# Modulation products on GpSimd and ScalarE beside the filter transforms, and the low parts of x on VectorE one product later

## The chip, the cores and the metric

The kernel runs on one core of one Trainium2 chip. The metric is the device time of one execution in microseconds (us); three timed runs of the kernel before gave a median of 2732.48 us (2732.22 to 2733.73). One further execution was recorded with the hardware profiler. The engines are named as the profile names them: PE is TensorE's matmuls, PEld its weight loads, DVE is VectorE, ACT is ScalarE, POOL is GpSimd (Pool), SP is SyncE, which issues most of the DMAs.

## What is computed

One block of a hybrid encoder on 512 tokens of width 2048, in float32. What matters here is its beginning: six modulation vectors from a condition, the first of which scale and shift the input; long filters that are made from positions; and the first projection.

```python
cond = silu(c)
mod  = cond @ w_ada + b_ada               # (2048) @ (2048 x 12288)
sh1, sc1, g1, sh2, sc2, g2 = split(mod, 6)
h = x * (1 + sc1) + sh1                   # 512 x 2048
z = h @ w_in + b_in                       # 2048 x 9216
# z feeds a spatial gating unit, a Hyena branch and two gates;
# the Hyena branch convolves with long filters
filt = hyena_filters(512, ...)            # a small MLP of sines, times a window
k_spec = spectrum(filt forward, filt backward)   # one for each of 2 orders
# then: branches, gates, w_o, layer norm, a 2048-8192-2048 MLP, layer norm
```

Only `sh1` and `sc1`, 2 x 2048 values, are needed before the first projection. Each value is a dot product of `cond` (2048) with a column of `w_ada`.

## The kernel before

**Products in three parts.** Large products are made as three products of 32-bit operands that are split in a high part and a low part: high times high, high times low, low times high. ScalarE rounds to the high part (`hi`), another engine subtracts it from the original to get the low part (`lo`). Weights are loaded in blocks of 128 x 1024 (512 KB), ScalarE makes `whi` (line 164, `cast`), VectorE makes `wlo` (line 169, `finish`). A block is 24 matmuls of 128 x 128 by 128 x 512.

**The modulation dot products.** `w_ada` is stored transposed, so that 128 outputs lie on the partitions and 1024 of the 2048 inputs along the row. An *item* is such a tile of 128 x 1024 (512 KB); a column group `kc` of 128 outputs needs four items (shift and scale, two halves each), and there are 16 groups, so 64 items before the first projection is complete. `Modulation.load` issues the DMA of the next item into one of two kinds of buffer: up to eight "early" ones in the pool `actp`, which is shared with the modulated input and shrinks as that fills, and a ring of three (`araw`). `Modulation.step` takes the oldest item, multiplies it with `cond` and sums it up in one VectorE instruction (line 289), and issues one more load. After every fourth step `first_input` runs for the next `kc`: Pool adds the two halves and the bias (`mod_sum`, lines 295 and 296, 128 x 2 elements each), ScalarE makes the high part of the modulated input and the modulated input itself in place (lines 476 and 477, 128 x 512), and Pool subtracts the two to get the low part (line 478).

**The filters.** `flt` makes the spectra in eight iterations (the loop over `n`, lines 547 to 566). In iteration `n`, PE makes the taps of part `n+1` (`taps`, line 435, 12 to 14 matmuls into four PSUM banks) and then the transform of part `n` (lines 360 to 372, 12 matmuls into four banks). ScalarE copies one of these banks (line 362). VectorE multiplies the taps of `n+1` with a window (`windowed`, line 445, four instructions, one operand in PSUM) and then makes sums and differences of the transform (`sums`, lines 376 to 381, six instructions, one operand in PSUM). With all eight banks in use, the taps of part `n+2` have to wait for `windowed(n+1)`, and the transform of `n+1` for `sums(n)`. In iterations 0, 2 and 4 `parts` splits the next filter weights, the low part on VectorE (line 77, 128 x 512). In each iteration VectorE also does two modulation steps, so that 20 of the 64 items are done when the loop ends.

**The first projection.** The loop over `u` (lines 574 to 591, 16 blocks of `w_in`) then interleaves, in VectorE's order, three or four modulation steps, the `wlo` of the next block (`finish`), and on PE the 24 matmuls of the present block, until at `u` = 12 all 64 items are done. After it come the short convolutions (lines 487 to 491) and the rest of the block, where PE works with little idle time to the end.

**The order.** Nothing is reordered: every engine and every DMA queue carries out its instructions in the order in which the program issues them, and waits on semaphores for the operands and buffers of each. An instruction that waits holds up all behind it on its engine.

Of the kernel before, what the change touches and what calls it, by code (L numbers as in the profile page):

```python
# [13 lines left out]
AF = mybir.ActivationFunctionType  # L14
OP = mybir.AluOpType
# [25 lines left out]
def block_kernel(ctx: ExitStack, tc: tile.TileContext, t):  # L41
    nc = tc.nc
# [11 lines left out]
    def slot(name, dt=F32):  # L54
        return heap.tile([P, 512], dt, name=name, tag="slot")
# [4 lines left out]
    def act_pair(kc):  # L60
        both = actp.tile([P, 1024], F32R, name=f"act{kc}", tag="act")
        return both[:, 0:512], both[:, 512:1024]
# [4 lines left out]
    def f32(ap):  # L67
        return ap.bitcast(F32)

    def load(dst, src, queue=nc.sync):  # L70
        queue.dma_start(dst, src)
        return dst
# [39 lines left out]
    class Weights:  # L112


        def __init__(self):
            self.blocks = blocks()
            self.raw, self.half, self.ready, self.kept, self.used = [], [], [], {}, set()
            self.ahead, self.done, self.later, self.queue = 1, False, None, nc.sync
# [12 lines left out]
        def load(self):  # L131
            w, cg, kp = next(self.blocks, (None, 0, 0))
            if w is None:
                self.done = True
                return
            raw = wts.tile([P, 1024], F32, name="wraw", tag="wraw")
            load(raw, w[cg, kp], self.queue)
            self.raw.append((raw, (w.name, cg, kp)))
# [96 lines left out]
    def cload(name, shape, queue=nc.sync):  # L235
        return load(const.tile(list(shape), F32, name="c_" + name), t[name], queue)
# [3 lines left out]
    nc.scalar.activation(warm, warm, AF.Sigmoid)  # L240
    hw1 = cload("hw1", (EMB, HID))
    featT = load(slot("featT")[:EMB], t["featT"])
    cond = const.tile([P, D], F32, name="cond")
    for h in range(2):
# [22 lines left out]
    dots = const.tile([P, 6, KC, 2], F32, name="dots")  # L267
    mod = const.tile([P, 6, KC], F32, name="mod")

    class Modulation:  # L270
        def __init__(self, order, room=lambda: 0):

            self.order, self.raw, self.room = [(m, kc, h) for m, kc in order for h in range(2)], [], room

        def load(self):
            early = sum(r[0] for r in self.raw)
            more = early < min(self.room(), 8)
            if self.order and (more or len(self.raw) - early < 3):
                m, kc, h = self.order.pop(0)
                if more:  # L280
                    raw = actp.tile([P, 1024], F32, name="araw", tag="act")
                else:
                    raw = wts.tile([P, 1024], F32, name="araw", tag="araw")
                load(raw, t["ada"][m, kc, h])
                self.raw.append((more, raw, m, kc, h))

        def step(self):
            _, raw, m, kc, h = self.raw.pop(0)
            nc.vector.scalar_tensor_tensor(raw, raw, 1.0, cond[:, 1024 * h:1024 * (h + 1)], op0=OP.mult,  # L289
                                           op1=OP.mult, accum_out=dots[:, m, kc, h:h + 1])  # L290
            if len(self.raw) < 11:
                self.load()

    def mod_sum(m, kc, eng=nc.vector):
        eng.tensor_tensor(mod[:, m, kc], dots[:, m, kc, 0], dots[:, m, kc, 1], op=OP.add)
        eng.tensor_tensor(mod[:, m, kc], mod[:, m, kc], bada[:, m, kc], op=OP.add)
# [47 lines left out]
    class Forward:  # L344
# [30 lines left out]
        def sums(self, tiles):  # L375
            nc.vector.tensor_tensor(self.ea, self.e0, self.eo, op=OP.add)
            self.minus(self.e0, self.e0, self.eo)
            for half, e in enumerate((self.ea, self.e0)):
                o = self.o[half]
                nc.vector.tensor_tensor(tiles[half], e, o, op=OP.add)  # L380
                self.minus(tiles[2 + half], e, o)
# [86 lines left out]

    h1 = []

    def first_input(kc, xt):

        mod_sum(slice(0, 2), kc, nc.gpsimd)
        hi, lo = act_pair(kc)
        sc, sh = mod[:, 1, kc:kc + 1], mod[:, 0, kc:kc + 1]
        nc.scalar.activation(hi, xt, AF.Identity, bias=sh, scale=sc)
        nc.scalar.activation(xt, xt, AF.Identity, bias=sh, scale=sc)
        nc.gpsimd.tensor_tensor(lo, xt, f32(hi), op=OP.subtract)
        h1.append((hi, lo))

    def short_conv(ps, which, hf):
# [16 lines left out]
    ada = Modulation(((m, kc) for kc in range(KC) for m in range(2)), lambda: KC - 2 - len(h1) - 4 * bool(windows))  # L498
# [14 lines left out]
    xt = []  # L513

    def x_load():
        if len(xt) < KC:
            xt.append(load(slot("xT"), t["xT"][len(xt)]))

    done = []

    def ada_steps(n):

        for _ in range(n):
            ada.step()
            done.append(None)
            if len(done) % 4 == 0:
                first_input(len(h1), xt[len(h1)])
                x_load()

    x_load()  # L530
    ada.load()
    fc = table("fwd", 3)
    for m in (1, 4):
        nc.vector.tensor_scalar(bada[:, m], bada[:, m], 1.0, None, op0=OP.add)
    busy(14)
    ada_steps(2)
    flt.parts(0)
    flt.ready()
    busy(14)
    x_load()  # L540
    for _ in range(5):
        ada.load()
    flt.taps(0)
    ada_steps(2)
    flt.windowed(0)
    weights.later, weights.queue = [], nc.scalar
    for n in range(8):
        if n < 6 and n % 2 == 0:
            flt.fetch(n + 2)
        if n < 7:  # L550
            flt.taps(n + 1)
        sums = flt.transform(n)
        ada_steps(2)
        if n < 7:
            flt.windowed(n + 1)
        flt.store()
        if n < 6:
            flt.parts(n + 2)
        sums()
        if 2 <= n < 5:  # L560
            weights.load()
        if n == 5:
            weights.cast()
        if n == 6:
            weights.finish()
            weights.cast()
# [198 lines left out]
    ada = Modulation((m, kc) for m in (2, 4, 3, 5) for kc in range(KC))  # L765
# [77 lines left out]
    for hf in range(2):  # L843
# [5 lines left out]
        for i in range(4):  # L849
            u, n = slot("u"), 4 * hf + i  # L850
# [70 lines left out]
    r = [[None] * 4 for _ in TILES]  # L921
# [103 lines left out]
    early, late = (0, 1), (2, 3)  # L1025
# [213 lines left out]
```

## Time and profile before

| | |
|---|---|
| median of the runs | 2732.48 us |
| the profiled execution's own time | 2733.2 us |
| its span, first to last instruction | 2731.4 us |
| PE busy | 2688.6 us (98%) |
| VectorE busy | 1539.5 us (56%) |
| ScalarE busy | 777.8 us (28%) |
| Pool busy | 118.8 us (4%) |
| mean granted TensorE clock | 0.996 |

The profile's rows give times in us from the start of the span. A row of a timeline reads: start, duration, engine, line, operation, output from inputs, partitions x elements and type, and how many such instructions the row merges; in brackets how long the engine was idle before it and what ended that. A row of the table by stages gives each engine's busy time in the stretch with the count of instructions, the granted clock, and the share and rate of the DMA engines. The shares over the whole span hide that the first 200 us, where the change lies, are limited in another way than the rest.

### The profile page before, as it was taken

The numbers are of one execution on the slowest core, as the hardware profiler recorded it, in microseconds if no ns is written. First come the engines' busy times: TensorE is split into PE (matmuls) and PEld (weight loads), VectorE is DVE, ScalarE is ACT, GpSimd is POOL, SyncE is SP. The second block draws the span as 40 slices with busy tenths as digits, with TensorE's granted clock in tenths as the row PEclk, the third lists the DMA queues.
The fourth block names the chain that finished last, engine by engine and source line by source line (L and its number), as shares of the span: only waits on it lengthen the run. The fifth ranks groups of instructions, "written<-read, shape, count | busy, mean of one in ns | idle before, by whom it ended". The sixth has DMA issues, their size and how long they took to land.

```text
span 2731.4 us, 30019 instructions
## 1 busy us (share of the span) xinstructions
PE 2688.6 (98%) x12019; PEld 2210.1 (81%) x12019; DVE 1539.5 (56%) x2052; ACT 777.8 (28%) x949; POOL 118.8 (4%) x102
## 2 busy tenths in 40 slices
PE   8999999999999999999999999999999999999996
PEld 5678778888888888878988888888888888888885
DVE  8987989544575566456774343443433434334348
ACT  2343332222232222324621222312223222131232
POOL 0330000000000000140010000000000000000001
PEclk9999999999999999999999999999999999999998
DMA  9762333555665567445543222322223222223342
GB/s 346 300 242 84 118 113 135 196 190 196 200 209 186 198 220 258 156 152 177 183 134 100 94 100 93 101 93 100 94 99 97 96 100 93 101 92 101 95 140 82
DMA packets 120189, 400.49 MB, mean 147 GB/s; under 512 B 14187, under 2 KB 14283, under 8 KB 119920
## 3 DMA queue, kind: packets, MB, share of 16 engines
q1 hardware_dynamic: 116656, 387.26, 41.9%
q10 hardware_dynamic: 3392, 11.31, 1.1%
q8 instruction: 94, 1.54, 0.2%
q14 instruction: 47, 0.39, 0.0%
HBM read 388.01 MB, written 10.50 MB: 146 GB/s over the span
## 4 chain that ended last, share of the span: by engine, by line
PE 91%; DVE 5%; DMA 3%; issue 1%; ACT 1%; SPq 0%; DVEq 0%; ACTq 0%
PE d L207 57%; PE t L952 29%; DMA araw<-in_ada 2%; PE flt L435 1%; PE f_o L338 1%; DVE wlo L169 1%; DMA spec<-spec 1%; PE inv L703 1%; PE inv L690 1%; DMA wraw<-in_w_m 0%; PE f L342 0%; DVE araw L289 0%; DVE r L1104 0%; DVE r L968 0%; PE tr L609 0%
## 5 line engine op out<-in xcount | busy, mean ns | idle before, releaser
L207 PE MATMUL d<-act,whi 128*128 128x512 f32 (+1 forms) x4224 | 1273.1, 384 | 0.0
L169 DVE TENSOR_TENSOR wlo<-wraw,whi 128x1024 fp32r<-128x1024 f32 x480 | 589.0, 1229 | 993.2 <-ACT whi L164 989.9
L164 ACT CAST whi<-wraw 128x1024 fp32r<-128x1024 f32 x480 | 504.9, 1053 | 1488.2 <-PE d L207 873.2
L207 PEld LDWEIGHTS d<-act,whi 128*128 128x128 f32 x4224 | 783.1, 188 | 155.6 <-issue 2.4
L207 PE MATMUL d<-act,wlo 128*128 128x512 f32 (+1 forms) x2112 | 810.2, 384 | 10.2 <-DVE wlo L169 10.2
L207 PEld LDWEIGHTS d<-act,wlo 128*128 128x128 f32 x2112 | 396.7, 188 | 93.3 <-DVE wlo L169 15.9
L952 PE MATMUL t<-whi,fh 128*128 128x512 f32 x960 | 373.5, 389 | 0.0
L952 PE MATMUL t<-wlo,fh 128*128 128x512 f32 x960 | 373.5, 389 | 0.0
L952 PE MATMUL t<-whi,fl 128*128 128x512 f32 x960 | 373.5, 389 | 0.0
L289 DVE SCALAR_TENSOR_TENSOR araw<-araw,cond 128x1024 f32<-128x1024 f32 x192 | 238.6, 1259 | 7.8 <-DMA araw<-in_ada 7.6
L952 PEld LDWEIGHTS t<-whi,fl 128*128 128x128 f32 x960 | 180.2, 188 | 37.4
L952 PEld LDWEIGHTS t<-whi,fh 128*128 128x128 f32 x960 | 180.2, 188 | 37.4
L952 PEld LDWEIGHTS t<-wlo,fh 128*128 128x128 f32 x960 | 180.2, 188 | 37.4
L952 PE MATMUL t<-whi,act 128*128 128x512 f32 x512 | 159.7, 391 | 0.0
L952 PEld LDWEIGHTS t<-whi,act 128*128 128x128 f32 x512 | 96.1, 188 | 19.9
L967 DVE TENSOR_TENSOR gated<-t,cond 128x512 f32<-128x512 f32 x126 | 86.2, 684 | 31.6 <-PE t L952 31.6
L952 PE MATMUL t<-wlo,act 128*128 128x512 f32 x256 | 99.8, 390 | 2.1 <-DVE wlo L169 2.1
L968 DVE TENSOR_TENSOR r<-r,gated 128x512 f32<-128x512 f32 x126 | 87.2, 692 | 4.3
L207 PE MATMUL d<-whi,act 128*128 128x512 f32 x256 | 79.0, 389 | 0.0
L1062 DVE TENSOR_TENSOR relu<-relu 128x512 f32<-128x512 f32 (+1 forms) x68 | 45.6, 671 | 38.2 <-ACT fh L1061 38.2
L1106 POOL TENSOR_TENSOR r<-r,ln2b 128x512 f32<-128x512 f32 x6 | 10.0, 1665 | 1305.1 <-DVE r L1104 1303.8
L952 PEld LDWEIGHTS t<-wlo,act 128*128 128x128 f32 x256 | 48.1, 188 | 12.3 <-DVE wlo L169 2.5
(253 smaller groups left out, 1966.9 us busy)
## 6 DMA issues: line engine op xcount, KB each, us to landing
wraw<-in_w_m SPq DMA_DIRECT2D x264, 512.0 KB, 3.5
araw<-in_ada SPq DMA_DIRECT2D x192, 512.0 KB, 5.7
wraw<-in_w_in SPq DMA_DIRECT2D x123, 512.0 KB, 3.6
wraw<-in_w_o SPq DMA_DIRECT2D x48, 512.0 KB, 3.4
spec<-spec SPq DMA_DIRECT2D x48, 256.0 KB, 4.0
wraw<-in_w_in ACTq DMA_DIRECT2D x21, 512.0 KB, 6.7
wraw<-in_w_b SPq DMA_DIRECT2D x16, 512.0 KB, 3.6
wraw<-in_w_a SPq DMA_DIRECT2D x16, 512.0 KB, 3.4
```

Source lines behind the costliest of these rows:

```text
L164: nc.scalar.copy(hi, raw)
L169: nc.vector.tensor_tensor(lo, raw, f32(hi), op=OP.subtract)
L207: nc.tensor.matmul(out[i], a, b, start=first and m == 0, stop=last and m == 2)
L289: nc.vector.scalar_tensor_tensor(raw, raw, 1.0, cond[:, 1024 * h:1024 * (h + 1)], op0=OP.mult, op1=OP.mult, accum_out=dots[:, m, kc, h:h + 1])
L338: nc.tensor.matmul(ps, fc(k), x, start=first, stop=last)
L435: nc.tensor.matmul(ps, a[:, cl, :], w, start=m == 0, stop=m == 2 and not extra)
L690: nc.tensor.matmul(ps, ic(4 * cs + COLUMN[cl]), y[cl][cs], start=(cs == 0), stop=(cs == 1))
L703: nc.tensor.matmul(ps[:, cl * P:(cl + 1) * P], conv.y[cl][cs][:, s], ic(4 * cs + COLUMN[cl]), start=(cs == 0), stop=(cs == 1))
L952: nc.tensor.matmul(out[i], a, b, start=kc == 0 and m == 0, stop=kc == 2 * pairs - 1 and m == 2)
L967: nc.vector.tensor_tensor(x, ps[i], g2_row[c], op=OP.mult)
L968: nc.vector.tensor_tensor(r[i][c], r[i][c], x, op=OP.add)
L1062: nc.vector.tensor_tensor(x, x, x, op=OP.mult)
```

## The change

Within the filter loop the two modulation steps on VectorE are taken out. In their place Pool makes the products of two or three items (`products`, 128 x 1024, in place), and at the head of the next iteration ScalarE sums each of them along its row (`add_up`, an activation with an accumulated output) and issues the next load. Ahead of the loop two items go to Pool and two more to VectorE. In all 19 items go through Pool and ScalarE and six through VectorE, 25 where 20 were done when the loop ends; the remaining 39 are VectorE steps in the loop over `u`, three to a block. Where the fourth item of a group was counted in `add_up`, `mod_sum` runs on VectorE; elsewhere it stays on Pool. The low part of the modulated input is now made on VectorE for all 16 groups: in the filter loop behind `windowed`, in the loop over `u` behind the next modulation step. An item that waits for `add_up` still counts against the buffers (`self.half`).

```diff
         def load(self):
-            early = sum(r[0] for r in self.raw)
+            early = sum(r[0] for r in self.raw + self.half)
             more = early < min(self.room(), 8)
-            if self.order and (more or len(self.raw) - early < 3):
+            if self.order and (more or len(self.raw + self.half) - early < 3):
...
+        def products(self, n):
+            for _ in range(n):
+                _, raw, m, kc, h = item = self.raw.pop(0)
+                nc.gpsimd.tensor_tensor(raw, raw, cond[:, 1024 * h:1024 * (h + 1)], op=OP.mult)
+                self.half.append(item)
+
+        def add_up(self):
+            n = len(self.half)
+            while self.half:
+                _, raw, m, kc, h = self.half.pop(0)
+                nc.scalar.activation(raw, raw, AF.Copy, accum_out=dots[:, m, kc, h:h + 1])
+                if len(self.raw) < 11:
+                    self.load()
+            return n
...
-    def first_input(kc, xt):
-        mod_sum(slice(0, 2), kc, nc.gpsimd)
+    lows = []
+    def low():
+        while lows:
+            lows.pop(0)()
+
+    def first_input(kc, xt, eng):
+        mod_sum(slice(0, 2), kc, eng)
         hi, lo = act_pair(kc)
         sc, sh = mod[:, 1, kc:kc + 1], mod[:, 0, kc:kc + 1]
         nc.scalar.activation(hi, xt, AF.Identity, bias=sh, scale=sc)
         nc.scalar.activation(xt, xt, AF.Identity, bias=sh, scale=sc)
-        nc.gpsimd.tensor_tensor(lo, xt, f32(hi), op=OP.subtract)
+        lows.append(lambda: nc.vector.tensor_tensor(lo, xt, f32(hi), op=OP.subtract))
         h1.append((hi, lo))
...
+    def counted(n, eng):
+        for _ in range(n):
+            done.append(None)
+            if len(done) % 4 == 0:
+                first_input(len(h1), xt[len(h1)], eng)
+                x_load()
+
     def ada_steps(n):
+        if not n:
+            low()
         for _ in range(n):
             ada.step()
-            done.append(None)
-            if len(done) % 4 == 0:
-                first_input(len(h1), xt[len(h1)])
-                x_load()
+            low()
+            counted(1, nc.gpsimd)
...
     flt.taps(0)
     ada_steps(2)
+    ada.products(2)
+    ada_steps(2)
+    low()
     flt.windowed(0)
     weights.later, weights.queue = [], nc.scalar
     for n in range(8):
         if n < 6 and n % 2 == 0:
             flt.fetch(n + 2)
+        counted(ada.add_up(), nc.vector)
         if n < 7:
             flt.taps(n + 1)
         sums = flt.transform(n)
-        ada_steps(2)
         if n < 7:
+            ada.products(2 + n % 2)
             flt.windowed(n + 1)
+        low()
         flt.store()
         if n < 6:
             flt.parts(n + 2)
```

More of the change, by code (lines that the diff above doesn't have):

```diff
@@ L271, in __init__ @@
         def __init__(self, order, room=lambda: 0):
-            self.order, self.raw, self.room = [(m, kc, h) for m, kc in order for h in range(2)], [], room
+            self.order, self.raw, self.half, self.room = [(m, kc, h) for m, kc in order for h in range(2)], [], [], room
         def load(self):
-            early = sum(r[0] for r in self.raw)
+            early = sum(r[0] for r in self.raw + self.half)
             more = early < min(self.room(), 8)
-            if self.order and (more or len(self.raw) - early < 3):
+            if self.order and (more or len(self.raw + self.half) - early < 3):
                 m, kc, h = self.order.pop(0)
```

## Prediction

> **What bounds the kernel now.** I read the shares of the chain that ended last, then the table by stages, then the timelines of DVE, PE and Pool in the first 200 us.
>
> ```profile
> PE 91%; DVE 5%; DMA 3%; issue 1%; ACT 1%; SPq 0%; DVEq 0%; ACTq 0%
> ...
> 40.00:50.00 10.00, 10.00 (x31) 6.01 (x30) 9.67 (x17) 3.21 (x5) 1.40 (x2) 1.00 1.01 371
> ...
> 100.00:120.00 20.00, 18.74 (x80) 14.93 (x81) 20.00 (x27) 6.97 (x9) 9.86 (x9) 1.00 1.03 410
> ...
> 140.00:160.00 20.00, 19.09 (x81) 14.59 (x79) 18.79 (x28) 7.54 (x9) 11.28 (x8) 1.00 1.03 406
> ```
>
> PE bounds nearly the whole span, so a gain or loss of the first 200 us is carried to the end. In these, two engines are full at once: in the filter loop PE (10.00 of 10) and DVE (9.67), in the loop over `u` DVE (20.00 of 20) and the DMA engines (share 1.03). Now one iteration of the filters on PE and on DVE:
>
> ```profile
> 47.40 1.02 PE L338 MATMUL f_ee<-flt,fwd 128*128 128x512 f32 x2
> ...
> 56.74 1.02 PE L338 MATMUL f_ee<-flt,fwd 128*128 128x512 f32 x2
> ...
> 91.91 1.02 PE L207 MATMUL d<-act,whi 128*128 128x512 f32 x2
> ```
> ```profile
> 45.98 1.22 DVE L289 SCALAR_TENSOR_TENSOR araw<-araw,cond 128x1024 f32<-128x1024 f32 x1
> ...
> 48.27 2.48 DVE L445 TENSOR_TENSOR flt<-flt,win 128x512 f32<-128x512 f32 x4
> 50.67 0.68 DVE L77 TENSOR_TENSOR w3l<-w,w3h 128x512 fp32r<-128x512 f32 x1
> 51.27 0.68 DVE L376 TENSOR_TENSOR bf_ea<-bf_e,f_eo 128x512 f32<-128x512 f32 x1
> ...
> 54.98 1.22 DVE L289 SCALAR_TENSOR_TENSOR araw<-araw,cond 128x1024 f32<-128x1024 f32 x1
> ...
> 96.35 1.22 DVE L289 SCALAR_TENSOR_TENSOR araw<-araw,cond 128x1024 f32<-128x1024 f32 x1
> ...
> 173.08 1.22 DVE L169 TENSOR_TENSOR wlo<-wraw,whi 128x1024 fp32r<-128x1024 f32 x1
> ```
>
> From start to start, DVE takes 1.145 us for a step (45.98 to 48.27 for two), 2.40 for `windowed`, 0.60 for a 128x512 subtraction, 3.71 for `sums`: 9.0 us in an iteration with the split, 8.4 without. PE takes 9.3 (47.40 to 56.74) and turns to the projection at 91.91. DVE reaches its first step of the loop over `u` at 96.35 and ends the `wlo` of block 13, behind the last item, at 174.3. Block 13 then releases PE:
>
> ```profile
> 174.36 8.70 PE d L207 x37
> ```
>
> **The port.** Pool and DVE exclude each other in some instructions:
>
> ```profile
> 22.65 0.20 POOL L295 TENSOR_TENSOR mod<-dots 128x2 f32<-128x2 f32 x1 [20.79 <-DVE araw L289]
> ...
> 42.71 1.27 POOL L478 TENSOR_TENSOR act<-xT,act 128x512 fp32r<-128x512 f32 x1 [2.58 <-ACT xT L477]
> ...
> 106.26 1.60 POOL L478 TENSOR_TENSOR act<-xT,act 128x512 fp32r<-128x512 f32 x1 [1.78 <-ACT xT L477]
> ```
> ```profile
> 43.20 0.68 DVE L380 TENSOR_TENSOR spec<-bf_ea,f_o 128x512 f32<-128x512 f32 x1
> ...
> 106.64 2.31 DVE L289 SCALAR_TENSOR_TENSOR araw<-araw,cond 128x1024 f32<-128x1024 f32 x1
> ```
> ```profile
> 1156.89 3.51 POOL L936 TENSOR_TENSOR r<-r,row 128x512 f32<-128x512 f32 x2
> 1156.97 2.29 DVE L169 TENSOR_TENSOR wlo<-wraw,whi 128x1024 fp32r<-128x1024 f32 x1 [4.21 <-ACT whi L164]
> ```
>
> At 106.64 both inputs of the DVE instruction lie in SBUF; it takes 2.31 us in place of 1.22, its last 1.1 behind Pool's end at 107.86. At 43.20 one input lies in PSUM, and neither waits. At 1156.97 DVE comes between two Pool instructions of 1.28: they take turns, so DVE waits for at most one Pool instruction.
>
> **The change, part by part.**
>
> *Two steps an iteration leave DVE.* That frees 2.29 us an iteration, but PE is full as well and cannot turn to the projection before 91.9. The last `sums` end some 1.7 us later, at 93.6. Alone this is worth 96.35 - 93.6 = 2.7 us.
>
> *Nineteen products on Pool.* No row has Pool at 128x1024. From 0.20 at 2 and 1.27 at 512 elements it is 2.34 us; bounds are 1.27 and, twice the row, 2.54. The Trainium skill (GPSIMD Engine Reference, "Reconciling with measured numbers") has 4497 ns for 2048 elements, an estimate of 2.25 us here; with that the sum would be some 0.7 us less. Pool has nothing between the products and waits only for the data, so from 24 us (steps 0 to 3, then `mod_sum`) it works without pause: 19 x 2.34 = 44.5 us and some 6 of turns, to about 75.
>
> *What DVE then waits for.* `windowed` and `sums` read PSUM and pass freely. Not so the subtraction behind `windowed`, the split in iterations 0, 2 and 4, and `mod_sum`, of which each of the two instructions (0.2 us) must take a turn. I take half a product (1.2) where DVE comes at any moment and a whole one (2.34) where it comes straight behind its last turn. Before the loop: step, product, low part, product, step, then `windowed(0)`, which ends at 32.9. Iteration 0: `mod_sum` 1.4 + 2.5, `windowed` 2.4, low part 1.8, split 2.9, `sums` 3.7: to 47.6. Iteration 1 has none: 6.1, to 53.7. Iteration 2 as iteration 0: to 68.4, where before it was 54.98. Iteration 3: 74.5. Then Pool is done: iteration 4 takes 9.0 (one last product), 5 takes 7.1, 6 takes 7.2 with the first `wlo`: 97.8. In iteration 7 `mod_sum` (0.4), the low part behind ScalarE (2.4, below) and `sums` (3.7) lead to 104.3. PE, with five more pieces of 2.8 to 5.2 behind `sums(3)`, is through at about 101 and does not end last. So the loop over `u` begins at 104.3 in place of 96.35, **8 us later**. The ends: with no wait at all 93.6 (2.7 earlier), with a whole product each time 109 (12.7 later).
>
> *The sums on ScalarE.* No row has one with an accumulator; bounds are a 128x1024 cast, 1.05 us, and two 128x512 activations, 1.64. Three at 1.64 are 4.9 us at the head of an iteration, in which ScalarE was busy for 3.21 of 10 us; the copy of `f_ee` and the split queue behind them and behind `mod_sum`, still ahead of DVE's `sums`. I cost this at nothing; its cover is `windowed`.
>
> *Loads.* SP issues them from `add_up` now. Counted through `load`, 33 are issued by the loop's end instead of 29, and one more of x.
>
> ```profile
> SPq L71 <- DVE araw L289: 22.0, 4, 18.7
> ```
>
> SP's wait of 18.7 us was for the buffer of step 19; the ring's items are now freed by `add_up` in iteration 5. The spec stores ahead of loads in SP's order wait for later `sums`, so loads 19 to 21 come later, though still ahead of Pool's need. The four items and the x tile, 2.36 MB, are 5.8 us at 406 GB/s. They count only if the DMA ends last.
>
> *The low part one product later.* Before, DVE did not wait for it; it lost Pool's turns.
>
> ```profile
> 102.22 1.11 POOL L295 TENSOR_TENSOR mod<-dots 128x2 f32<-128x2 f32 x1 [5.87 <-DVE araw L289]
> 103.42 1.07 POOL L296 TENSOR_TENSOR mod<-mod,c_bada 128x2 f32<-128x2 f32 x1
> ```
> ```profile
> 104.52 0.82 ACT L476 ACTIVATE act<-xT,mod 128x512 fp32r<-128x512 f32 x1 [8.61 <-POOL mod L296]
> 105.37 0.82 ACT L477 ACTIVATE xT<-xT,mod 128x512 f32<-128x512 f32 x1
> ```
> ```profile
> 96.35:174.30 77.95, 70.36 (x298) 54.57 (x296) 74.84 (x104) 26.92 (x31) 40.52 (x32) 1.00 0.98 384
> ...
> L289 DVE SCALAR_TENSOR_TENSOR araw<-araw,cond 128x1024 f32<-128x1024 f32 x44 | 59.8, 1395 | 2.6 <-DMA araw<-in_ada 2.4
> ```
>
> A fourth item ends at t. Pool's first addition waits behind DVE's next step, to t + 1.2; the second finds DVE waiting and takes 0.2; ScalarE's pair takes 1.7; the low part can start at t + 3.3. DVE stands at it from t + 1.15: **a stall of 2.1 us**, behind which the next steps and `wlo` queue, and PE behind these. Where the fourth item is the third of its block, `wlo` lies between and it is 1.8. Nine low parts come ahead of block 13's `wlo`: 6 x 2.1 + 3 x 1.8 + 9 x 0.6 = 23.4 us. With 39 x 1.145 + 13 x 1.14 + 0.4 for the two of `cb` that makes 83.3 us in place of 77.95, **5.3 us more**: five steps fewer (-5.7), no more Pool turns or waits for data (-12.4 = 77.95 less 65.6 of work), and 23.4. The bounds: 74.2 if Pool's and ScalarE's chain hides (-3.7), 86 if ScalarE's casts fall ahead of it in every second case (+8). Per block this is 6.4 us, against 5.6 for PE (24 at 8.70/37) and 5.7 for the DMA (2.3 MB), so DVE ends last.
>
> **The sum**, on the profiled execution: 2733.2 + 8 + 5.3 = 2746.5; the median of the runs is 0.7 lower: **2746**.
>
> **The rivals.**
>
> *The turns cost little (2735).* Pool's products find DVE mostly at instructions that read PSUM. Then the loop over `u` begins 2.7 early and is 5.3 longer: +2.6. Speaks for it: DVE's bare work drops by 2.3 us an iteration. Against: the row at 106.64, and that Pool has always a product ready.
>
> *The loads decide (2727, faster).* If the DMA, full in the loop over `u`, ends last both before and after, stalls of DVE fall into waits for data and the 2.36 MB fetched earlier are a gain: -5.8. It decides if DVE's time per block stays under 5.7 us. For it: share 1.03 at 100 to 160 us. Against: of 77.95 us DVE waited 2.4 for data.
>
> *PE's clock falls (2755).* The waits open gaps of 3 to 4 us on PE in iterations 0 to 3.
>
> ```profile
> 19.60 0.62 PE L435 MATMUL flt<-w3h,a2eh 128*128 128x512 f32 x1 [3.03 <-ACT a2eh L76]
> ...
> 22.00:24.00 2.00, 2.00 (x4) 1.21 (x4) 1.25 (x3) 0.82 (x1) 0.39 (x2) 0.50 1.04 416
> ...
> 26.00:28.00 2.00, 2.00 (x6) 1.53 (x6) 1.41 (x3) 0.00 (x0) 0.17 (x1) 0.50 1.04 416
> ```
>
> After a gap of 3.03 us the granted clock was 0.50 from 22 to 28. Half the pace for 6 us costs 3 us, three such falls 9. The Trainium skill (TensorE: Matmul & The Clock Gate, "Part 1: The HAM clock gate") says that the clock halves after an idle window of about 3.4 us; by that rule some of the gaps would do it, and the row agrees.
>
> **How the numbers follow.** A measurement of this kernel can tell about 0.2%, 5.5 us. My forecast has 0.58, the small turns 0.16, the loads 0.12, the clock 0.12; 0.02 is left, slower too. So faster 0.12, same 0.16, slower 0.72. The likeliest alone spans 2738 to 2752; the range of 2733 to 2757 leaves out the loads' case and little above.
>
> **What would show it.** Pool busy some 45 us more; DVE subtractions and `mod_sum` in the filter loop at 1.5 to 3 us instead of 0.2 to 0.7; the first step over `u` near 104; DVE idle for 2 us before nearly each low part there, with ScalarE as releaser; block 13's `wlo` near 187.6. If low parts start without a wait, or the first step over `u` comes before 97, I am wrong.

## The result, and the profile after

The changed kernel takes 2758.9 us (median of four runs, 2757.89 to 2761.32), beside 2733.1 for the kernel before on the same chip: a ratio of 1.0093, 95% interval 1.0076 to 1.0111. It is slower, as forecast, but by 26 us and not by 13: 2746 was predicted, and the time lies 2 us above the range.

The profiled execution takes 2759.61 us, 26.4 more than that of before. Two stretches hold 25.0 of it: the filter loop, at whose end the first step over `u` now stands at 116.64 in place of 96.35 (20.3 us), and the loop over `u`, 82.6 us in place of 77.95 (4.7). VectorE's timeline of the changed kernel: among others the first instruction of each of the iterations 0 to 7 (`mod_sum` or `windowed`), then rows of the loop over `u`.

```profile
35.07 2.22 DVE L311 TENSOR_TENSOR mod<-dots 128x2 f32<-128x2 f32 x1
37.32 2.27 DVE L312 TENSOR_TENSOR mod<-mod,c_bada 128x2 f32<-128x2 f32 x1
39.52 2.47 DVE L461 TENSOR_TENSOR flt<-flt,win 128x512 f32<-128x512 f32 x4
41.91 2.85 DVE L500 TENSOR_TENSOR act<-xT,act 128x512 fp32r<-128x512 f32 x1
44.68 2.82 DVE L77 TENSOR_TENSOR w3l<-w,w3h 128x512 fp32r<-128x512 f32 x1
...
51.13 0.68 DVE L461 TENSOR_TENSOR flt<-flt,win 128x512 f32<-128x512 f32 x1
...
56.29 0.69 DVE L392 TENSOR_TENSOR bf_ea<-bf_e,f_eo 128x512 f32<-128x512 f32 x1 [1.10 <-PE f_eo L354]
...
60.85 1.04 DVE L311 TENSOR_TENSOR mod<-dots 128x2 f32<-128x2 f32 x1
...
73.59 0.68 DVE L461 TENSOR_TENSOR flt<-flt,win 128x512 f32<-128x512 f32 x1
...
83.79 0.16 DVE L311 TENSOR_TENSOR mod<-dots 128x2 f32<-128x2 f32 x1
...
91.75 0.16 DVE L311 TENSOR_TENSOR mod<-dots 128x2 f32<-128x2 f32 x1
...
101.09 2.48 DVE L461 TENSOR_TENSOR flt<-flt,win 128x512 f32<-128x512 f32 x4
...
110.19 0.16 DVE L311 TENSOR_TENSOR mod<-dots 128x2 f32<-128x2 f32 x1
...
116.64 1.22 DVE L289 SCALAR_TENSOR_TENSOR araw<-araw,cond 128x1024 f32<-128x1024 f32 x1
...
124.22 0.69 DVE L500 TENSOR_TENSOR act<-xT,act 128x512 fp32r<-128x512 f32 x1 [1.77 <-ACT xT L499]
...
198.06 1.22 DVE L169 TENSOR_TENSOR wlo<-wraw,whi 128x1024 fp32r<-128x1024 f32 x1
```

The turns are there, and up to the end of iteration 0 (51.13) they are nearly whole: an addition of 128 x 2, which takes 0.16 alone (83.79), holds VectorE for 2.22, and a subtraction of 0.68 for 2.85. The Trainium skill (SBUF — State Buffer, "Who interferes with whom") has it that a VectorE instruction with two inputs in SBUF and a GpSimd instruction that reads SBUF exclude each other for the whole of the first; the rows agree. PE's timeline and the stages show more: within the filter loop PE stands, and its clock falls.

```profile
33.41 2.08 PE L354 MATMUL f_ee<-flt,fwd 128*128 128x512 f32 x2 [3.50 <-DVE flt L461]
...
47.56 0.82 PE L451 MATMUL flt<-w3l,a2eh 128*128 128x512 f32 x1 [4.56 <-DVE w3l L77]
...
70.02 0.63 PE L451 MATMUL flt<-w3l,a2eh 128*128 128x512 f32 x1 [2.21 <-DVE w3l L77]
```
```profile
44.00:54.00 10.00, 6.44 (x12) 3.74 (x13) 8.75 (x11) 0.42 (x2) 10.00 (x5) 0.51 0.33 111
...
70.00:77.00 7.00, 6.99 (x14) 4.41 (x15) 5.62 (x9) 0.00 (x0) 2.19 (x1) 0.56 0.53 184
...
92.31:101.09 8.78, 8.78 (x27) 5.99 (x28) 7.22 (x11) 6.13 (x10) 0.00 (x0) 1.00 0.27 98
101.09:110.19 9.10, 9.10 (x25) 4.80 (x25) 7.47 (x12) 3.62 (x6) 0.00 (x0) 1.00 0.72 263
...
116.64:199.28 82.64, 70.36 (x294) 55.32 (x293) 66.06 (x103) 25.99 (x30) 14.59 (x19) 0.98 0.83 297
```

Columns: window and length, busy time of PE, PEld, DVE, ACT and POOL, granted clock, DMA share, GB/s. The taps of part 2 need the low part of the filter weights (`w3l`, line 77), which VectorE splits as the last of its turns; PE waits 4.56 us for it, and the clock is 0.51 from 44 to 54. In the last row the loop over `u` takes 82.64 us, where 83.3 were forecast, with VectorE busy for 66.06; the waits of VectorE there are headed by

```profile
DVE act L500 <- ACT xT L499: 16.5, 9, 2.1
```

16.5 us in nine waits, 18.0 were forecast. Behind this loop nothing is given back: the first `hz` of ScalarE, which ends a long wait for the projection, comes 25.9 us later than before.

```profile
208.97 0.69 ACT L509 ACTIVATE hz<-d,c_bin 128x512 f32<-128x512 f32 x1 [5.76 <-PE d L207]
```
```profile
183.08 0.69 ACT L487 ACTIVATE hz<-d,c_bin 128x512 f32<-128x512 f32 x1 [4.86 <-PE d L207]
```

(The second is the row of the kernel before.)

### The profile page after: what moved, and what is told of

Its sections match the earlier page's. It is cut to its first block, busy times and chain, and to the rows that moved or that the text cites. A ratio compares the mean times of both kernels' runs of the same rounds, so it can differ in the third digit from the quotient of the medians.

```text
span 2757.5 us, 30026 instructions
## 1 busy us (share of the span) xinstructions
PE 2698.4 (98%) x12019; PEld 2214.4 (80%) x12019; DVE 1543.0 (56%) x2040; ACT 797.7 (29%) x987; POOL 132.2 (5%) x95
## 4 chain that ended last, share of the span: by engine, by line
PE 89%; DVE 6%; DMA 2%; issue 1%; ACT 1%; POOL 0%; SPq 0%; DVEq 0%; ACTq 0%; POOLq 0%
PE d L207 57%; PE t L986 28%; DVE araw L289 1%; DMA araw<-in_ada 1%; DVE wlo L169 1%; PE flt L451 1%; PE f_o L354 1%; PE inv L737 1%; PE inv L724 0%; DMA wraw<-in_w_m 0%; PE f L358 0%; DMA xT<-in_xT 0%; DVE r L1138 0%; DVE r L1002 0%; PE tr L643 0%
## 5 line engine op out<-in xcount | busy, mean ns | idle before, releaser
L289 DVE SCALAR_TENSOR_TENSOR araw<-araw,cond 128x1024 f32<-128x1024 f32 x173 | 212.9, 1244 | 5.5 <-DMA araw<-in_ada 5.1
L986 PEld LDWEIGHTS t<-wlo,act 128*128 128x128 f32 x256 | 48.1, 188 | 12.3 <-DVE wlo L169 2.5
```

What stands on the lines that cost most here:

```text
L986: nc.tensor.matmul(out[i], a, b, start=kc == 0 and m == 0, stop=kc == 2 * pairs - 1 and m == 2)
```

## The experiments

Below, "first step" is the start of VectorE's first step over `u` (before 96.35, after 116.64), "u loop" the time from there to the end of the `wlo` of block 13 (before 77.95, after 82.6). Ratios are to runs of the kernel before on the same chip, whose medians were 2734.8 to 2735.2.

| kernel | us | ratio, 95% interval | first step | u loop |
|---|---|---|---|---|
| e1_lo_only | 2749.86 | 1.0055 (1.0040 to 1.0070) | 98.14 | 92.8 |
| e2_products_only | 2731.49 | 0.9986 (0.9976 to 0.9995) | 98.42 | 70.1 |
| e3_lo_late | 2748.34 | 1.0044 (1.0027 to 1.0060) | 118.97 | 67.8 |
| e4_half_products | 2742.88 | 1.0031 (1.0019 to 1.0043) | 100.31 | 82.6 |
| e5_no_w3_low | 2748.38 | 1.0051 (1.0037 to 1.0065) | 104.71 | 82.5 |
| e6_warm | 2754.31 | 1.0072 (1.0058 to 1.0086) | 110.74 | 82.5 |
| e7_pool_waits | 2752.18 | 1.0066 (1.0053 to 1.0080) | 110.47 | 82.6 |
| e8_products_wlo_first | 2732.23 | 0.9990 (0.9981 to 0.9999) | 99.41 | |
| e9_products_cast_first | 2731.82 | 0.9988 (0.9979 to 0.9997) | 99.62 | |
| e10_before_cast_first | 2735.74 | 1.0001 (0.9992 to 1.0010) | | |
| e11_gated | 2743.28 | 1.0032 (1.0020 to 1.0044) | 99.44 | 82.6 |
| e12_gated_late | 2731.86 | 0.9990 (0.9980 to 0.9999) | 100.42 | 66.9 |

**Each part alone.** e1 is the kernel before with only the low parts moved to VectorE.

```diff
-        nc.gpsimd.tensor_tensor(lo, xt, f32(hi), op=OP.subtract)
+        lows.append(lambda: nc.vector.tensor_tensor(lo, xt, f32(hi), op=OP.subtract))
...
             ada.step()
+            low()
```

> The kernel before with only the low part of x moved to VectorE, one modulation step later; no products on Pool. My theory (in the loop over u VectorE stands about 2.1 us at each low part): 44 steps x 1.145 + 13 wlo x 1.14 + 10 low parts x 2.65 = 92 us from the first step of that loop to the end of block 13's wlo, where the kernel before has 78; the filter loop is unchanged (first step of the loop over u at 96 to 97). Time some 14 us above the kernel before, 2747. Rival (the low part costs its own 0.6 us and saves Pool's turns, all that is lost is lost in the filter loop): 72 to 78 us, time 2727 to 2733.

The loop over `u` grows to 92.8 us, and in its waits VectorE stands ten times for ScalarE (us in total, times, longest):

```profile
DVE act L484 <- ACT xT L483: 19.7, 10, 2.1
```

The stall is real: the low part's move alone costs 0.55%. (The first step comes 1.8 us later, so a small part of that lies in the filter loop.) The rival that the DMA hides the stall is out.

e2 is the changed kernel with the low parts on Pool again, as before.

```diff
-        lows.append(lambda: nc.vector.tensor_tensor(lo, xt, f32(hi), op=OP.subtract))
+        nc.gpsimd.tensor_tensor(lo, xt, f32(hi), op=OP.subtract)
```

> The changed kernel with the low part of x back on Pool, where it stands in Pool's queue ahead of the next products. My theory (Pool's products hold VectorE up in the filter loop): the first step of the loop over u still comes late, at 103 to 114, less than the 116.6 of the changed kernel since Pool now has to wait for ScalarE between products; the loop over u then takes 69 to 74 us (five steps fewer, no stall): 2740 to 2750. Rival (the stall at the low part is what costs, in the filter loop too): first step before 98, time 2722 to 2730.

The loop over `u` came out as expected, but the filter loop did not: 98.42, hardly later than before, with the same 19 products on Pool. The timelines of Pool and VectorE in e2 say why:

```profile
35.00 1.27 POOL L500 TENSOR_TENSOR act<-xT,act 128x512 fp32r<-128x512 f32 x1 [3.35 <-ACT xT L499]
36.23 12.19 POOL L298 TENSOR_TENSOR araw<-araw,cond 128x1024 f32<-128x1024 f32 x5
```
```profile
32.86 0.16 DVE L311 TENSOR_TENSOR mod<-dots 128x2 f32<-128x2 f32 x1 [4.64 <-ACT araw L305]
...
35.94 0.88 DVE L77 TENSOR_TENSOR w3l<-w,w3h 128x512 fp32r<-128x512 f32 x1 [0.32 <-ACT w3h L76]
```

Pool's low part waits for ScalarE, which waits for `mod_sum`, and all later products stand behind it in Pool's queue. So `mod_sum` and the split meet no product (0.16 and 0.88 in place of 2.22 and 2.82), and the products of iteration 0 start only at 36.23. The products as such thus cost little; it matters where in VectorE's order they run.

**What the turns cost.** In e4 Pool multiplies only the first 512 of an item's 1024 columns; the other half is summed up without its product.

```diff
-                nc.gpsimd.tensor_tensor(raw, raw, cond[:, 1024 * h:1024 * (h + 1)], op=OP.mult)
+                nc.gpsimd.tensor_tensor(raw[:, :512], raw[:, :512], cond[:, 1024 * h:1024 * h + 512], op=OP.mult)
```

> The changed kernel, with Pool multiplying only the first half (128x512) of each item; the second half is summed up unmultiplied. My theory (VectorE waits a whole Pool instruction at each turn): turns of 1.3 us in place of 2.3, some eleven turns in iterations 0 and 2, so the loop over u begins 10 to 14 us earlier, at 103 to 107: 2746 to 2749. Rival (the sums on ScalarE, in front of the copies, hold the loop up): they are the same length here, so the time stays within 3 us of the changed kernel.

The first step comes 16.3 us earlier, more than was expected, though ScalarE's sums are as many and as long. The timelines of VectorE and PE in e4:

```profile
31.66 1.28 DVE L311 TENSOR_TENSOR mod<-dots 128x2 f32<-128x2 f32 x1
...
37.09 0.68 DVE L77 TENSOR_TENSOR w3l<-w,w3h 128x512 fp32r<-128x512 f32 x1
...
100.31 1.22 DVE L289 SCALAR_TENSOR_TENSOR araw<-araw,cond 128x1024 f32<-128x1024 f32 x1
```
```profile
37.82 0.63 PE L451 MATMUL flt<-w3l,a2eh 128*128 128x512 f32 x1 [0.25 <-DVE w3l L77]
```

So most of the filter loop's loss is Pool's occupation of the port and what follows from it, not the sums on ScalarE. The loop over `u`, without products, stays at 82.6.

**PE's wait for the split weights.** In e5 the taps use the high part of the filter weights in place of the low part, which isn't made.

```diff
-                both = slot_pair("w3")
-                split(w, *both)
+                wh = slot("w3h", F32R)
+                nc.scalar.copy(wh, w)
+                both = wh, wh
```

> The changed kernel without the low parts of the filter weights of all four parts (the subtraction is left out, the taps use the high part in its place). Theory A (in iterations 0 and 2 PE stands at the taps for this subtraction, which VectorE reaches only after its turns, so that PE's work of the next iteration starts late, and cold, and comes behind VectorE's in place of beside it): besides a turn of 2.8 us in each of the two iterations the waits of the next ones go; first step of the loop over u at 102 to 107 in place of 116.6, time 2744 to 2750. Theory B (only the number of turns counts): two turns of 2.8 us less, first step at 110 to 112, time 2753 to 2755.

The first step moves from 116.64 to 104.71, as the theory has it. The edit removes the split's turns on VectorE with PE's wait, so the 11.9 us hold both.

In e6 idle transposes on PE fill the waits ahead of the taps of parts 2 and 4.

```diff
+                for _ in range(warm if cl == 0 else 0):
+                    nc.tensor.transpose(ps[:, :P], ident, ident)
...
-            flt.taps(n + 1)
+            flt.taps(n + 1, {1: 40, 3: 20}.get(n, 0))
```

> The changed kernel with idle transposes on PE ahead of the taps of parts 2 (40 of them) and 4 (20), in the stretches in which it waits for the low part of the filter weights. If the fall of PE's clock after these gaps costs (0.50 at 44 to 54 and 70 to 77 us): the clock stays at 1.0 there, the two following pieces are some 3 us shorter each, first step of the loop over u at 110 to 113, time 2752 to 2755. If the gaps alone cost: within 1 us of the changed kernel, first step at 116 to 117.

Two stages of e6 (columns as above), and the ends of its iterations 0 to 3 in VectorE's timeline:

```profile
43.00:48.00 5.00, 4.20 (x34) 3.89 (x32) 5.00 (x3) 1.33 (x4) 5.00 (x3) 1.00 0.00 0
48.00:54.00 6.00, 6.00 (x19) 3.75 (x19) 5.83 (x11) 1.24 (x2) 6.00 (x3) 1.00 0.54 185
```
```profile
51.08 2.47 DVE L463 TENSOR_TENSOR flt<-flt,win 128x512 f32<-128x512 f32 x4
...
58.26 0.93 DVE L311 TENSOR_TENSOR mod<-dots 128x2 f32<-128x2 f32 x1
...
69.23 0.68 DVE L463 TENSOR_TENSOR flt<-flt,win 128x512 f32<-128x512 f32 x1
...
77.89 0.71 DVE L311 TENSOR_TENSOR mod<-dots 128x2 f32<-128x2 f32 x1
```

The clock stays at 1.00, iteration 0 ends as in the changed kernel (51.08 beside 51.13), and 5.9 us are gained. Iteration 1 takes 7.2 us in place of 9.7: these 2.5 us are the clock's. Iterations 2 and 3 take 11.0 and 8.7 in place of 12.7 and 10.2, but there more than the clock changed: the second `mod_sum` instruction met no product this time, so that the split, done at 65.6, came ahead of the taps (66.92), and PE did not wait for it. So the clock's fall is part of the loss, 2.5 us and at most 5.9, and most of the loss is something else.

**The same products at another place.** In e7 a small Pool instruction that reads `xT` stands ahead of the products, to imitate what held them back in e2.

```diff
+        if eng is nc.vector:
+            nc.gpsimd.tensor_tensor(gate, xt[:, 0:2], xt[:, 2:4], op=OP.add)
```

> The changed kernel with one small instruction (128x2) on Pool ahead of the products of each iteration that ends a group; it reads the modulated input, so Pool waits there for ScalarE as it does for its low part in the kernel with the products alone. The low part itself stays on VectorE. Theory: what spared that kernel is the wait in Pool's queue, which lets mod_sum and windowed pass before the next product starts; here mod_sum needs no turn, the low part and the split still do. First step of the loop over u at 100 to 106, the loop over u as in the changed kernel (82 to 83 us): 2743 to 2749. Rival (it was spared because VectorE has one instruction less): first step at 112 to 116, time 2754 to 2758.

A miss, for the theory and for the rival: 110.47. VectorE's timeline in e7:

```profile
32.71 0.14 DVE L311 TENSOR_TENSOR mod<-dots 128x2 f32<-128x2 f32 x1
...
35.36 2.57 DVE L503 TENSOR_TENSOR act<-xT,act 128x512 fp32r<-128x512 f32 x1
37.85 2.83 DVE L77 TENSOR_TENSOR w3l<-w,w3h 128x512 fp32r<-128x512 f32 x1
```

`mod_sum` passes, but `xT` releases Pool and VectorE's low part at the same moment; the low part and the split take whole turns again, and PE again waits for the split (3.70 us).

In e11 the small instruction reads VectorE's last subtraction instead, and the products are issued behind it.

```diff
-            ada.products(2 + n % 2)
             flt.windowed(n + 1)
...
+            if last:
+                m = f32(last.pop())
+                nc.gpsimd.tensor_tensor(gate, m[:, 0:2], m[:, 2:4], op=OP.add)
+            ada.products(2 + n % 2)
         sums()
```

> The changed kernel with the same products on Pool and the same instructions on VectorE, but in each iteration the products stand behind a small Pool instruction (128x2) that reads VectorE's last subtraction of that iteration, so that they run beside sums and windowed, which read PSUM. Theory (the place of Pool's turns, not their amount, made the filter loop late): low part, split and mod_sum at 0.2 to 0.9 us except for one or two, no wait of PE for the split, clock 1.0 from 30 us on; first step of the loop over u at 98 to 102 in place of 116.6, the loop over u unchanged at 82 to 83 us, 2738 to 2744. Rival (19 products beside the filters are too many wherever they stand): first step after 108.

The timelines of Pool and of VectorE in e11:

```profile
36.67 0.20 POOL L601 TENSOR_TENSOR gate<-w3l 128x2 f32<-128x2 f32 x1 [7.43 <-DVE w3l L77]
36.81 11.75 POOL L298 TENSOR_TENSOR araw<-araw,cond 128x1024 f32<-128x1024 f32 x5
```
```profile
35.30 0.69 DVE L504 TENSOR_TENSOR act<-xT,act 128x512 fp32r<-128x512 f32 x1
35.90 0.69 DVE L77 TENSOR_TENSOR w3l<-w,w3h 128x512 fp32r<-128x512 f32 x1
...
47.42 1.17 DVE L311 TENSOR_TENSOR mod<-dots 128x2 f32<-128x2 f32 x1
...
99.44 1.22 DVE L289 SCALAR_TENSOR_TENSOR araw<-araw,cond 128x1024 f32<-128x1024 f32 x1
```

All 19 products and all sums are still made, and 17.2 of the 20.3 us are gone. Within the loop Pool begins behind VectorE's subtractions and runs beside `sums` and `windowed`, which read PSUM; only `mod_sum` still meets it (1.17). PE waits for no split there, and its clock is 1.00 from 30 to 100 us.

**The low part later.** In e3 the low parts of the loop over `u` come behind the third modulation step after their group in place of the first; e12 is e11 with the same edit.

```diff
-        while lows:
-            lows.pop(0)()
+        while lows and len(done) - lows[0][0] >= age:
+            lows.pop(0)[1]()
...
+    late[0] = 2
```

> The changed kernel, with the low part in the loop over u made three modulation steps later in place of one. My theory: no wait ahead of the low parts; VectorE's own work from the first step to block 13's wlo is 39 x 1.145 + 13 x 1.14 + 9 x 0.6 + 0.4 = 65.3 us, but the DMA (5.7 us a block) or PE (5.5) then end last, so 70 to 74 us in place of 82.6: 9 to 12 us below the changed kernel, 2747 to 2750. Rival (the waits at the low part only take the place of waits for data or PE): within 3 us of the changed kernel.

> The same with the low part in the loop over u three modulation steps later. Theory: both losses are gone; first step at 98 to 102, then some 68 us, where PE (16 blocks of 5.45 us from about 95) ends last: 2729 to 2734, no slower than the kernel before. If it stays above 2740, a third loss is left that I have not found.

The stage of e3's loop over `u`:

```profile
118.97:186.77 67.80, 65.35 (x281) 53.60 (x281) 65.57 (x103) 26.13 (x30) 17.15 (x19) 0.97 0.96 363
```

e3's loop over `u` takes 67.8 us, less than the 70 to 74 expected, and the kernel is 13.3 us above before in place of 25.8: the stall was the place in the order, not the subtraction. e12, with both causes away, is at 0.999 of before.

**What is left of the gain.** e2 ends its loop over `u` at 168.55, 5.8 us ahead of before, and gains 3.5. One wait of PE in it stood out; e8 moves the `wlo` of block 1 ahead of the first steps, e9 the cast of block 2 as well, and e10 makes e9's edit in the kernel before.

```diff
+        if u == 0:
+            weights.finish()
+            weights.cast()
         ada_steps(min(steps, (u + 1) * steps // 13) - len(done) + first)
-        weights.finish()
+        if u:
+            weights.finish()
```

> The kernel with the products on Pool and the low part on Pool, and in the loop over u the wlo of block 1 ahead of the first three modulation steps in place of behind them. In the kernel without that, PE waits 3.1 us for this wlo at 103 and is then busy without a gap to 180. Theory: PE is what ends last in the loop over u there, so the 3.1 us are a gain to the end: 2728 to 2729, some 0.2% below the kernel before. Rival (VectorE ends last): within 1 us of that kernel, 2731.

> The kernel with products and low part on Pool, with the wlo of block 1 and the cast of block 2 both ahead of the first three modulation steps of the loop over u. With the wlo alone ahead PE's wait of 3.1 us only moved to the next block, whose cast stood behind the modulated input on ScalarE. Theory: now neither waits, and PE, which had no other gap up to 180 us, is 3 us or more ahead: 2727 to 2729. Rival (VectorE or the DMA ends last from there on): within 1 us of 2731.5.

> The kernel before with the same reordering at the first block (wlo of block 1 and cast of block 2 ahead of the first modulation steps). There VectorE ends last in the loop over u (78 us for 66 us of work, Pool's turns and waits for data), so the reordering should give nothing: within 1.5 us of the kernel before. If it gains as much as it does with the products on Pool, that gain has nothing to do with the products.

The wait of 3.13 us at 103.12 in e2 only changes its name, first in e8, then in e9 (PE's timelines):

```profile
107.95 0.76 PE L207 MATMUL d<-act,whi 128*128 128x512 f32 x2 [3.07 <-ACT whi L164]
```
```profile
107.77 0.50 PE L207 MATMUL d<-act,wlo 128*128 128x512 f32 x1 [2.24 <-DVE wlo L169]
```

Neither is faster than e2, so the gains expected of e8 (2728 to 2729) and e9 (2727 to 2729) were both missed; e10 is as before. The 5.8 us are VectorE's lead, and in e2 VectorE no longer ends last: PE has no gap after the one at 103.12, and the first `hz`, which waits for PE, is 4.6 us ahead (178.52 beside 183.08). Between that and 3.5 the runs can't tell, as the interval of e2's ratio spans 1.4 to 6.6 us. Why the wait moves on instead of going away stays open.

## Why the prediction was wrong in size

*The step that failed* is the term "8 us later" for the filter loop: it measured 20.3, outside its own bound of 12.7. Within it, the sentence "PE, with five more pieces of 2.8 to 5.2 behind `sums(3)`, is through at about 101 and does not end last" was false where it matters. PE turned to the projection at 112.40:

```profile
112.40 1.03 PE L207 MATMUL d<-act,whi 128*128 128x512 f32 x2
```

VectorE did begin its first step after that, at 116.64, but its `sums` had waited for PE in iterations 1, 3, 5 and 6. The chain of work that ended last runs through PE from 47.56 to 59.6 and from 70.02 to about 105. The walk followed VectorE alone; it named gaps of 3 to 4 us on PE, but only in a rival and only for the clock, and put at nothing that PE's work behind such a gap comes later. Set beside the rows above (iterations from the start of one to that of the next):

| | predicted | measured |
|---|---|---|
| loop begins | 32.9 | 35.07 |
| iteration 0 | 14.7 | 16.06 |
| 1 | 6.1 | 9.72 |
| 2 | 14.7 | 12.74 |
| 3 | 6.1 | 10.20 |
| 4 | 9.0 | 7.96 |
| 5 | 7.1 | 9.34 |
| 6 | 7.2 | 9.10 |
| 7, to the first step | 6.5 | 6.45 |

Three errors make up the 12.3 us:

- *Turns.* I took half a product where VectorE comes at any moment. Ahead of the loop and in iteration 0 it met nearly whole ones: 3.5 us more by 51.13 (0.7 of them a wait for the data of a step). In iterations 2 and 4 it went the other way (1.04 and 0.16 for the first `mod_sum`): 3.0 less. That was luck: Pool, which was to have a product always ready, waited 10.7 us for data in between.
- *PE in iterations 1 and 3,* 7.7 us. I priced these at VectorE's bare 6.1 because no subtraction of SBUF lay in them. But the split ends VectorE's turns, the taps need it, and so PE's taps and transform came behind VectorE's work instead of beside it; VectorE then waited for PE (56.29). The clock's fall is 2.5 of the 3.6 us of iteration 1, by e6; its share of the 4.1 of iteration 3 is not known. e5, with no split to wait for and none to make, comes to 104.71.
- *PE in iterations 5 and 6,* 4.1 us: PE is busy for all of the 17.9 us from 92.31 to 110.19 at a clock of 1.00, while VectorE was forecast to set 7.1 and 7.2.

*The rival "PE's clock falls"* (2755, the forecast and 9 us) named a true mechanism at too high a price: 2.5 us are shown, 5.9 are the most. That its time came nearest to the 2758.9 is in part luck, as it holds neither PE's wait for the split nor PE's pace in iterations 5 and 6.

*The loop over `u`:* 83.3 predicted, 82.6 measured; 18.0 us of stalls, 16.5 measured; and 82.5 or 82.6 in the five experiments that leave this loop as it is (e4 to e7 and e11), whatever the filter loop did. The longest stall is the 2.1 us forecast. The rival "the loads decide" fell with e1, "the turns cost little" with the result; e11 shows that the latter holds if the products are put elsewhere.

*The products and the sums.* Pool's 19 products were predicted at 2.34 us, ScalarE's sums were bounded by 1.05 and 1.64 and costed at nothing. One product alone, the group of the 19, and the sums (fastest/mean/slowest in ns, of the changed kernel):

```profile
79.89 2.39 POOL L298 TENSOR_TENSOR araw<-araw,cond 128x1024 f32<-128x1024 f32 x1 [7.70 <-DMA araw<-in_ada]
```
```profile
L298 POOL TENSOR_TENSOR araw<-araw,cond 128x1024 f32<-128x1024 f32 x19 | 48.4, 2580 | 10.7 <-DMA araw<-in_ada 10.7
```
```profile
L305 ACT ACTIVATE araw<-araw x19: 1042/1048/1062, 25.6 to 106.0; 128x1024 f32<-128x1024 f32 x19
L305 ACT ACTIVATION_READ_ACCUMULATOR araw<-araw x19: 183/191/195, 26.6 to 107.0; 128x1 f32 x19
```

Both prices held. That the loads come ahead of Pool's need did not: the last product began at 79.89 and not before 75, and Pool's waits for data are the 10.7 us of the second row. The sums are all kept in e2, e4 and e11, where the first step comes 2.1 to 4.0 us after that of before; they cost at most a part of that.

## What to carry to other kernels

When work goes to an engine that shares a port, follow not only the engine that must take turns but the one that waits for its last instruction: a delay of a split by a few turns became a serial PE behind VectorE, and a lower clock on top. Price each small instruction that must take a turn at a whole instruction of the other engine, and let the port's other user start behind the short shared-port instructions, beside those that read PSUM (e11: the same work, and the filter loop ends 17 us earlier). A result handed over two engines needs that chain's time in the order of the engine that picks it up: one step later stalled 1.8 us on average and 2.1 at most, three steps later hardly cost anything (e3: VectorE busy 65.6 of 67.8 us). Even with both losses away (e12), and in e2, the move is worth only 0.10% to 0.14% here.

## What the runs showed of the hardware

- An addition of 128 x 2 on VectorE took 2.22 and 2.27 us between back-to-back products of Pool, 0.16 without. The length of the VectorE instruction hardly plays a part in its wait: 2.06 us more for this addition, 2.17 for a subtraction of 128 x 512 (2.85 in place of 0.68).
- A wait in Pool's own queue worked as protection: e2's low part, waiting 3.35 us for ScalarE, kept five products off the port until VectorE had passed. Taking the low part off Pool removed that wait and gave VectorE the subtractions instead. A wait put back on Pool for `mod_sum` (e7) returned 6.2 of the 20.3 us, one behind VectorE's last subtraction (e11) 17.2.
- With PE's wait of 4.56 us the clock was 0.51 from 44 to 54 us, the last 3.6 us of the wait and 6.44 us of work; transposes of no use in the wait kept it at 1.00 and made iteration 1 shorter by 2.5 us. The Trainium skill (TensorE: Matmul & The Clock Gate, "Part 1: The HAM clock gate") names an idle window of about 3.4 us; this wait was longer, and the row agrees. But shorter waits were followed by a lower clock too: 3.03 us in the kernel before (0.50 from 22 to 28), so that the row which the prediction set beside that rule agrees with it only roughly, and 2.21 us at 70.02 in the changed kernel (0.56 from 70 to 77). A wait of 2.23 us in e11, which ended at 30.99, was not (1.00 from 30 to 34). So 3.4 us is no safe bound for a gap here, and what decides for the shorter ones is not shown.
